# Sixty-four slots in a unit of its own for the fourth 128-slot expert, another order of the units, and biases added to the sum one unit later

## The chip, the cores and the metric

The kernel runs on one core of one Trainium2 chip, as one launch. The metric is the device time in microseconds (us); three runs of a kernel make a median. The profiled execution has its own time, and a span from its first to its last instruction.

## The reference, cut to what matters

One layer: a mixer (attention heads and a gated linear recurrence), a layer norm, then a mixture of 32 experts of which each token takes four, and a last layer norm. Sixteen meta tokens are prepended and dropped at the end, so the experts see 256 tokens here.

```python
def moe(h, w_router, b_router, w_gu, b_gu, w_dn, b_dn):
    logits = (h @ w_router) + b_router
    top_val, top_idx = lax.top_k(logits, TOP_K)          # 4 of 32
    gates = jax.nn.softmax(top_val, axis=-1)
    ...
    def expert_block(args):
        gu = xb @ w_gu[e] + b_gu[e]                      # 1024 -> 2048
        gate = jnp.minimum(gu[:, 0::2], SWIGLU_LIMIT)
        up = jnp.clip(gu[:, 1::2], -SWIGLU_LIMIT, SWIGLU_LIMIT)
        act = (up + 1.0) * gate * jax.nn.sigmoid(gate * SWIGLU_ALPHA)
        return act @ w_dn[e] + b_dn[e]                   # 1024 -> 1024
    ...
    return jnp.einsum('tkd,tk->td', y_assign, gates)
```

The weights are float32: 1024x2048 and 1024x1024 for each expert, 12.6 MB, or 403 MB for all 32.

## The kernel before

The mixer takes the first 200 us or so. Then come the experts, in a fixed list of units (`UNITS`). A place in that list is a rank: ranks 0 and 1 are experts 0 and 1 (their weights are fetched before the router is known), and ranks 2 to 31 are the other 30 experts sorted by how many tokens chose them, the fullest first. Each rank has a fixed number of slots, one for each token that chose it. A unit is 128 slots, shared by its ranks: one rank with 128 slots, two with 64 or four with 32. For a unit, `one_hots` builds a matrix of which token stands in which slot and gathers the tokens with matmuls (`gather`, L716), `slot_gates` weighs and transposes that matrix (L733), the experts run one after another (`expert128`, `expert64`, `expert32`), and in the next unit's first expert `combine` (L897, L898) adds the weighted result to the sum `acc`. Gather and slot gates of the next unit are issued inside the last expert of a unit.

Every expert reads its weights in six chunks of 2 MB, four for gate and up and two for down, and all chunks are issued from SP's queue in the order in which TensorE uses them (`chunk`, L310). They land in a ring of nine buffers, and an issue waits until TensorE has read the last of the chunk that held the buffer nine chunks earlier. So the transfers run up to nine chunks, one expert and a half, ahead of TensorE, and stop when TensorE falls too far behind. TensorE's order is the order of the program text; calls such as `amid.append((4, f))` put `f` after phase 4 of an expert (phases 0 to 3 are the four chunks of gate and up, 4 the activation, 5 the middle of down).

`begin_acc` allocates `acc`, multiplies the gates with the down biases of all experts (L981, four matmuls in the text, eight in the trace, since each float32 matmul is there twice) and adds the residual (L982). Before, it stands in the second expert of unit 0, after its third chunk.

`spread` brings the rows of the last norm's gain and bias, which `begin_acc` fetches on ACT's queue, to all partitions (two matmuls each); it stands in the last experts of units 12 and 13.

If more tokens chose an expert than it has slots (`C_CAP`, compared in `places`), a flag in `ordi` lets a loop behind the kernel's end (L1113) run such experts again with 128 slots, twice, and write the output again.

Of the kernel before, what the change touches and what calls it, by code (L numbers as in the profile page):

```python
# [16 lines left out]
OP = mybir.AluOpType  # L17
PSUM = mybir.MemoryType.PSUM if hasattr(mybir, "MemoryType") else bass.MemoryType.PSUM

P = 128  # L20
D = 1024
T = 256
# [18 lines left out]
C_CAP = C_SEL + 2 * 2  # L41
# [39 lines left out]
mix 0 4, split 35, close, prefetch 1, mix 0 5, mix 1 5, mix 0 6, mix 0 7, mix 1 6  # L81
"""


NS = 2
UNITS = [(0, 1), (28, 29, 30, 31), (2,), (18, 19), (16, 17), (3,), (14, 15), (24, 25, 26, 27), (4,), (12, 13), (10, 11),
         (5,), (8, 9), (20, 21, 22, 23), (6, 7)]


def constants():  # L90
    c = np.zeros((P, NC_CONST), np.float32)
    i = np.arange(P)
    c[:, C_ID:C_ID + P] = np.eye(P)
    c[:, C_TRI:C_TRI + P] = i[:, None] < i[None, :]
    c[:, C_ONE:C_ONE + P] = 1.0
    c[:, C_IOTA:C_IOTA + NE] = np.arange(NE)
    c[:, C_IOTA1:C_IOTA1 + P] = np.arange(1, P + 1)
    e = np.arange(NE)
    key = np.where(e < NS, 1e6 - e, NE - 1 - e)
    c[:, C_KC] = key[i % NE]  # L100
    c[:, C_KC + 1] = 6 * (i % NE)
    c[:, C_KR:C_KR + NE] = key
    for j in range(2):
        c[:, C_GRP + j] = i // NE % 2 == j
        for r in range(NS):
            c[:, C_SEL + j * NS + r] = (i // NE % 2 == j) & (i % NE == r)
    for unit in UNITS:
        for r in unit:
            c[:, C_CAP + r] = P // len(unit)
    x = np.zeros((P, NC_MIX), np.float32)  # L110
    rot = np.zeros((P, P), np.float32)
    for m in range(2):
        for j in range(32):
            rot[m * 64 + j, m * 64 + 32 + j] = -1.0
            rot[m * 64 + 32 + j, m * 64 + j] = 1.0
    x[:, E_ROT:E_ROT + P] = rot.T
    pos = np.arange(L, dtype=np.float32)
    inv = (1.0 / (np.float32(10000.0) ** (np.arange(0, 64, 2, dtype=np.float32) / np.float32(64)))).astype(np.float32)
    ang = (pos[:, None] * inv[None, :]).astype(np.float32)
    ang = np.concatenate([ang, ang, ang, ang], axis=1).T  # L120
    x[:, E_COS:E_COS + L] = np.cos(ang)
    x[:, E_SIN:E_SIN + L] = np.sin(ang)
    for lv, m in enumerate((1, 2, 4, 8, 16)):
        tt = np.arange(P).reshape(-1, 2, m)[:, 1].reshape(-1)
        x[:, E_MSK + lv * 64:E_MSK + lv * 64 + 64] = (
            (i[:, None] // (2 * m) == tt[None, :] // (2 * m)) & ((i[:, None] // m) % 2 == 0))
    return c, x


def build(ctx, tc, x, meta, consts_d, mixc_d, vecs_d, rows_d, win_d, wout_d, wr_d, br_d, bgu_d, bdn_d, wexp_d, out):  # L130
    nc = tc.nc
# [17 lines left out]
    def bank(tag):  # L149
        return ps.tile([P, 512], F32, name="ps_" + tag, tag=tag, bufs=4 if tag == "s" else 2)  # L150

    def t1(name, shape=(P, L), dt=F32):
        return cpool.tile(list(shape), dt, name=name, tag="t1", bufs=T1)

    def t4(name, shape=(P, D), dt=F32):
        return cpool.tile(list(shape), dt, name=name, tag="t4", bufs=T4)
# [535 lines left out]
        nc.vector.scalar_tensor_tensor(gat[:, a, :], ex, zz, msk[:, a, :], op0=OP.mult, op1=OP.mult)  # L692


    def hot(pc, n):

        w = P // n
        G = t1("G", (P, 2, n, w))
        nc.vector.tensor_tensor(G, con[:, None, None, C_IOTA1:C_IOTA1 + w].to_broadcast([P, 2, n, w]),  # L699
                                pc[:, :, :, None].to_broadcast([P, 2, n, w]), op=OP.is_equal)  # L700
        return G

# [4 lines left out]

    def gather(G, amid=None):

        XT = t4("XT", (P, KT, P))  # L710
        bs = [bank("s") for _ in range(2)]
        for a in range(2):
            if a and amid:
                amid()
            for k in range(KT):
                nc.tensor.matmul(bs[k // 4][:, k % 4 * P:(k % 4 + 1) * P], h[:, a, k * P:(k + 1) * P],  # L716
                                 G[:, a].rearrange("p n w -> p (n w)"), start=(a == 0 and k % 4 == 0),
                                 stop=(a == 1 and k % 4 == 3))
        for c in range(2):
            (nc.vector.tensor_copy if c else nc.scalar.copy)(XT[:, c * 4:(c + 1) * 4, :],  # L720
                                                             bs[c].rearrange("p (k s) -> p k s", s=P))
        return XT

    def gated(G, gc, n):
        Gg = t1("Gg", (P, 2, n, P // n))
        nc.vector.tensor_tensor(Gg, G, gc[:, :, :, None].to_broadcast([P, 2, n, P // n]), op=OP.mult)
        return Gg

    def turned(Gg):

        cb = bank("g")
        for a in range(2):
            nc.tensor.transpose(cb[:, a * P:(a + 1) * P], Gg[:, a].rearrange("p n w -> p (n w)"), ident)  # L733
        C = t1("C", (P, 2, P))
        nc.vector.tensor_copy(C, cb[:, 0:T].rearrange("p (a t) -> p a t", a=2))
        return C

    def swiglu(gu):
        g = t1("g", (P, 256))
# [14 lines left out]
        nc.vector.tensor_copy(at, tr[:, 0:256].rearrange("p (c s) -> p c s", c=2))  # L754
        return at

    def bias_of(src, n):

        t = t1("sel", (P, 256), F32R)
        k = 6 if n == 4 else 2  # L760
        src = src[:, 2:4] if k == 2 and src.shape[1] == 6 else src
        nc.gpsimd.tensor_copy(t[:, 0:k * P // n].rearrange("p (j w) -> p j w", j=k), src.to_broadcast([P, k, P // n]))  # L762
        return t[:, 0:k * P // n]

    def expert64(X, Y, u, w, sel, amid=()):

# [123 lines left out]

    def combine(C, Y):
        acc = late["both"]
        for a in range(2):
            for c in range(2):
                cs = slice(c * 512, (c + 1) * 512)
                o = bank("s")
                nc.tensor.matmul(o, C[:, a, :], Y[:, cs], start=True, stop=True)  # L897
                nc.vector.tensor_tensor(acc[:, a, cs], acc[:, a, cs], o, op=OP.add)  # L898

    def dynamic(e6, parts=1):  # L900
        return lambda i: chunk(wexp_d[bass.ds(e6 + i, 1)].rearrange("a p c -> p (a c)"), parts if i > 2 else 1)
# [98 lines left out]
    total, Cs, Ys, Gs = {}, {}, {}, {}  # L1000
    coming = {0: XT}

    def one_hots(i):
        us = slice(UNITS[i][0], UNITS[i][0] + len(UNITS[i]))
        Gs[i] = hot(psms[:, :, us], len(UNITS[i]))
        coming[i] = gather(Gs[i])

    def slot_gates(i):
        us = slice(UNITS[i][0], UNITS[i][0] + len(UNITS[i]))
        Cs[i] = turned(gated(Gs[i], gats[:, :, us], len(UNITS[i])))  # L1010

    def weigh_first():
        for a in range(2):
            weigh(a)
        Gs[0] = gated(G, gat[:, :, 0:2], 2)

    def turn_first():
        gates_turn()
# [13 lines left out]

    def choose_bias(i, r):
        src = con[:, C_SEL:C_SEL + 2 * NS].rearrange("p (j r) -> p j r", j=2) if r < NS else sels
        chosen[r] = bias_of(src[:, :, r:r + 1], len(UNITS[i]))

    line = [(i, r) for i, unit in enumerate(UNITS) for r in unit]
    choose_bias(*line.pop(0))
    end = len(UNITS) - 1
    for i, unit in enumerate(UNITS):  # L1040
        XT = coming.pop(i)
        Ys[i] = t4("Y")
        for u, r in enumerate(unit):
            amid = []
            if u == 0 and i:
                amid.append((4, lambda: combine(Cs.pop(i - 1), Ys.pop(i - 1))))
            if u == 0 and i == end:
                amid.append((5, begin_total))
            if u and i == end:
                amid.append((6, lambda: end_total(0)))  # L1050
            if i in (end - 2, end - 1) and u == len(unit) - 1:
                amid.append((3, lambda: spread(i - end + 2)))
            if i == 0:
                amid += ([(0, places), (0, weigh_first), (1, turn_first), (2, places_turn), (3, sort)] if u == 0 else
                         [(2, begin_acc)])
            if u == len(unit) - 1 and i < end:
                amid += [(4, lambda: one_hots(i + 1)), (5, lambda: slot_gates(i + 1))]
            sel = chosen.pop(r)
            if line:
                j, q = line.pop(0)  # L1060
                choose_bias(j, q)
            if len(unit) == 4:
                expert32(XT, Ys[i], u, weights(r), sel, amid)
            elif len(unit) == 2:
                expert64(XT, Ys[i], u, weights(r, 4 if i == end and u else 1), sel, amid)
            else:
                expert128(XT, Ys[i], weights(r), sel, amid)
# [45 lines left out]
    with tc.If(anyv > 0):  # L1113
        with tc.For_i(0, NE, 1) as r:
            ovr = nc.values_load(ordi[0:1, bass.ds(r + NE, 1)], min_val=0, max_val=1)
            with tc.If(ovr > 0):
# [8 lines left out]
                for base in (0, P):  # L1125
                    if base:
                        nc.vector.tensor_scalar(pc, pc, float(-base), None, op0=OP.add)
                    G = hot(pc, 1)
                    XT = gather(G)
                    C = turned(gated(G, gc, 1))  # L1130
                    Y = t4("Y")
                    expert128(XT, Y, dynamic(e6), bias_of(sc, 1))
                    combine(C, Y)
        finish(lambda a, c: acc[:, a, c * 512:(c + 1) * 512])

# [43 lines left out]
```

## Time and profile before

| | us |
|---|---|
| median of 3 runs | 1148.9 (1145.93 to 1151.4) |
| time of the profiled execution | 1149.03 |
| span of the profiled execution | 1146.9 |
| TensorE busy with matmuls | 1028.2 |
| transfers, mean over the span | 374 GB/s |

The span lacks 2.1 us of the execution's own time. The profiled execution is 0.1 us over the median. Times inside the trace count from the span's start.

### The profile page before, as it was taken

How to read it: one execution, taken by the hardware profiler on the slowest of the kernel's cores; microseconds unless marked ns; L12 is line 12 of the kernel's file. 1: busy time of each engine (PE TensorE's matmuls, PEld its weight loads, DVE VectorE, ACT ScalarE, POOL GpSimd, SP SyncE). 2: the span in 40 equal slices, each digit the busy share in tenths (PEclk: the TensorE clock that was granted, in tenths of full speed). 3: DMA queues.
4: the chain of work that ended last, by engine and by line, in shares of the span. 5: the costliest groups of instructions: out<-in, count | busy, mean ns of one | idle time of the engine just before them, and what ended most of it. 6: DMA issues, size and time to landing. Idle time of an engine off the chain costs nothing.

```text
span 1146.9 us, 14789 instructions
## 1 busy us (share of the span) xinstructions
PE 1028.2 (90%) x6040; PEld 536.5 (47%) x6041; DVE 343.2 (30%) x736; ACT 177.4 (15%) x393; POOL 99.3 (9%) x91
## 2 busy tenths in 40 slices
PE   5999898999679999999999767999999999966995
PEld 5988777443224544444444323444445534422442
DVE  6685878221101321212222101222121321200124
ACT  4424463101000001110001100000101001100102
POOL 3653314000000000000000000000000000000000
PEclk9989999999889999999999888999999999977998
DMA  6653468989999999999799999999999989999994
GB/s 215 263 219 111 148 220 311 377 361 402 427 427 427 428 427 428 427 427 428 311 429 427 426 427 427 429 427 427 428 428 426 410 327 429 427 428 426 427 420 162
DMA packets 37022, 428.44 MB, mean 374 GB/s; under 512 B 4388, under 2 KB 4772, under 8 KB 12758
## 3 DMA queue, kind: packets, MB, share of 16 engines
q1 hardware_dynamic: 36322, 426.71, 89.5%
q8 instruction: 50, 0.82, 0.3%
q10 hardware_dynamic: 628, 0.74, 0.2%
q14 instruction: 22, 0.18, 0.0%
HBM read 426.38 MB, written 1.05 MB: 373 GB/s over the span
## 4 chain that ended last, share of the span: by engine, by line
PE 69%; DMA 16%; DVE 6%; ACT 1%; issue 1%; POOL 0%; DVEq 0%; ACTq 0%; POOLq 0%
PE ps_pj L779 19%; DMA wchunk<-in_wexp 16%; PE ps_pj L793 10%; PE ps_s L828 5%; PE ps_pj L836 5%; PE ps_pj L828 5%; PE ps_s L716 5%; PE ps_pj L864 4%; PE ps_pj L320 4%; PE ps_s L897 2%; PE ps_pj L876 2%; DVE acc L898 1%; PE ps_s L409 1%; PE ps_g L752 1%; PE ps_pj L774 1%
## 5 line engine op out<-in xcount | busy, mean ns | idle before, releaser
L779 PE MATMUL ps_pj<-wchunk,XT 128*64 128x512 f32 x1024 | 230.5, 597 | 1.1 <-DMA wchunk<-in_wexp 1.1
L742 DVE TENSOR_SCALAR g<-ps_pj 128x256 f32<-128x256 f32 x52 | 22.0, 424 | 507.8 <-PE ps_pj L864 222.5
L864 PE MATMUL ps_pj<-wchunk,XT 128*32 128x512 f32 x768 | 116.2, 707 | 41.0 <-DMA wchunk<-in_wexp 41.0
L779 PEld LDWEIGHTS ps_pj<-wchunk,XT 128*64 128x64 f32 x1024 | 69.2, 137 | 131.9 <-issue 129.7
L793 PE MATMUL ps_pj<-wchunk,at 128*64 128x256 f32 x1024 | 116.4, 382 | 1.1 <-DVE at L754 1.1
L743 ACT ACTIVATE sgm<-g 128x256 f32<-128x256 f32 x60 | 25.0, 417 | 524.2 <-DVE g L742 516.4
L793 PEld LDWEIGHTS ps_pj<-wchunk,at 128*64 128x64 f32 x1024 | 71.3, 137 | 40.2 <-issue 3.3
L320 PE MATMUL ps_pj<-c,whi 128*128 128x272 f32 (+1 forms) x420 | 87.2, 302 | 0.7 <-DVE c L242 0.4
L864 PEld LDWEIGHTS ps_pj<-wchunk,XT 128*32 128x32 f32 x768 | 28.0, 125 | 122.0 <-issue 65.8
L762 POOL CAST sel<-sels 128x128 fp32r<-128x128 f32 (+2 forms) x30 | 10.6, 352 | 856.9 <-DVE up L746 218.5
L716 PE MATMUL ps_s<-G,h 128*128 128x128 f32 x480 | 57.8, 278 | 15.3 <-DVE G L699 14.0
L320 PEld LDWEIGHTS ps_pj<-c,whi 128*128 128x128 f32 x420 | 70.3, 199 | 2.5 <-DVE c L242 0.8
L716 PEld LDWEIGHTS ps_s<-G,h 128*128 128x128 f32 x480 | 54.8, 192 | 27.4 <-DVE G L699 24.4
L876 PE MATMUL ps_pj<-wchunk,at 128*32 128x256 f32 x768 | 56.8, 440 | 10.7 <-issue 6.2
L320 PE MATMUL ps_pj<-c,wlo 128*128 128x272 f32 (+1 forms) x224 | 65.9, 294 | 0.0
L181 POOL TENSOR_TENSOR wlo<-wraw,whi 128x1024 fp32r<-128x1024 f32 x20 | 51.4, 2570 | 61.3 <-ACT whi L179 61.2
L836 PE MATMUL ps_pj<-wchunk,at 128*128 128x512 f32 x128 | 56.3, 592 | 0.0
L828 PE MATMUL ps_s<-wchunk,XT 128*128 128x512 f32 x128 | 55.6, 592 | 0.0
L828 PE MATMUL ps_pj<-wchunk,XT 128*128 128x512 f32 x128 | 55.6, 592 | 0.0
L897 PE MATMUL ps_s<-Y,C 128*128 128x512 f32 x112 | 51.4, 602 | 0.0
L179 ACT CAST whi<-wraw 128x1024 fp32r<-128x1024 f32 x36 | 37.6, 1047 | 61.5 <-PE ps_pj L320 23.5
L876 PEld LDWEIGHTS ps_pj<-wchunk,at 128*32 128x32 f32 x768 | 29.4, 126 | 34.4 <-issue 17.3
(293 smaller groups left out, 966.6 us busy)
## 6 DMA issues: line engine op xcount, KB each, us to landing
wchunk<-in_wexp SPq DMA_DIRECT2D x189, 2048.0 KB, 21.7
wraw<-in_win SPq DMA_DIRECT2D x28, 512.0 KB, 3.7
wchunk<-in_wexp SPq DMA_DIRECT2D x12, 512.0 KB, 18.6
wraw<-in_wout SPq DMA_DIRECT2D x8, 512.0 KB, 5.5
h<-in_x SPq DMA_DIRECT2D x4, 256.0 KB, 3.1
braw<-in_bgu SPq DMA_DIRECT2D x1, 512.0 KB
eg<-in_rows SPq DMA_DIRECT2D x1, 512.0 KB, 4.5
eb<-in_rows SPq DMA_DIRECT2D x1, 512.0 KB
```

The costliest lines, as they stand in the source:

```text
L179: nc.scalar.copy(hi, raw)
L181: eng.tensor_tensor(lo, raw, hi.bitcast(F32), op=OP.subtract)
L320: nc.tensor.matmul(b[:, 0:n], w[:, ks], v[:, L - n:L], start=(k == 0 and j == 0), stop=(k == KT - 1 and j == 2))
L716: nc.tensor.matmul(bs[k // 4][:, k % 4 * P:(k % 4 + 1) * P], h[:, a, k * P:(k + 1) * P], G[:, a].rearrange("p n w -> p (n w)"), start=(a = ...
L743: nc.scalar.activation(sgm, g, AF.Sigmoid, scale=1.702)
L779: nc.tensor.matmul(gu[ab * 64:(ab + 1) * 64, :], X[:, kh * 4 + k, u * SL:(u + 1) * SL], wv[:, k, ab * 512:(ab + 1) * 512], start=False, st ...
L793: nc.tensor.matmul(dn[c][ab * 64:(ab + 1) * 64, 0:256], aTs[f // 4][:, f % 2, f // 2 % 2 * 64:f // 2 % 2 * 64 + 64], wv[:, f, ab * 256:(ab ...
L828: nc.tensor.matmul(gus[ab], X[:, kh * 4 + k, :], wv[:, k, ab * 512:(ab + 1) * 512], start=False, stop=(kh == 1 and k == 3))
L836: nc.tensor.matmul(dn[c], aT[f // 2][:, f % 2, :], wv[:, f, :], start=(f == 0), stop=(f == KT - 1))
L864: nc.tensor.matmul(gu[q * 32:(q + 1) * 32, :], X[:, kh * 4 + k, us], wv[q // 2][:, k, q % 2 * 512:(q % 2 + 1) * 512], start=False, stop=(k ...
L876: nc.tensor.matmul(dn[q * 32:(q + 1) * 32, 0:256], at[:, f % 2, f // 2 * 32:(f // 2 + 1) * 32], wv[q // 2][:, f, q % 2 * 256:(q % 2 + 1) * ...
L897: nc.tensor.matmul(o, C[:, a, :], Y[:, cs], start=True, stop=True)
```

## The change

`UNITS` now names the slots of each rank apart from how many ranks are in the unit. Rank 5, the fourth fullest of the sorted ones, had 128 slots and now has 64, alone in its unit; that unit's other 64 slots do not exist, so gather, transposes and combine work on 64 rows or columns. The units stand in another order, and `begin_acc` moves to the first expert of unit 1, ahead of that expert's `combine`.

```diff
-UNITS = [(0, 1), (28, 29, 30, 31), (2,), (18, 19), (16, 17), (3,), (14, 15), (24, 25, 26, 27), (4,), (12, 13), (10, 11),
-         (5,), (8, 9), (20, 21, 22, 23), (6, 7)]
+UNITS = [(64, (0, 1)), (32, (28, 29, 30, 31)), (128, (2,)), (64, (18, 19)), (64, (16, 17)), (64, (14, 15)), (64, (12, 13)),
+         (64, (5,)), (64, (10, 11)), (128, (3,)), (64, (8, 9)), (32, (24, 25, 26, 27)), (128, (4,)),
+         (32, (20, 21, 22, 23)), (64, (6, 7))]
...
-    for unit in UNITS:
-        for r in unit:
-            c[:, C_CAP + r] = P // len(unit)
+    for w, unit in UNITS:
+        c[:, C_CAP + np.array(unit)] = w
...
+        ns = G.shape[2] * G.shape[3]
...
-                nc.tensor.matmul(bs[k // 4][:, k % 4 * P:(k % 4 + 1) * P], h[:, a, k * P:(k + 1) * P],
+                nc.tensor.matmul(bs[k // 4][:, k % 4 * P:k % 4 * P + ns], h[:, a, k * P:(k + 1) * P],
...
-                nc.tensor.matmul(o, C[:, a, :], Y[:, cs], start=True, stop=True)
+                nc.tensor.matmul(o, C[:, a, :], Y[0:C.shape[0], cs], start=True, stop=True)
...
             if i == 0:
-                amid += ([(0, places), (0, weigh_first), (1, turn_first), (2, places_turn), (3, sort)] if u == 0 else
-                         [(2, begin_acc)])
+                amid += [(0, places), (0, weigh_first), (1, turn_first), (2, places_turn), (3, sort)] if u == 0 else []
+            if i == 1 and u == 0:
+                amid.insert(0, (2, begin_acc))
...
-            if len(unit) == 4:
+            if w == 32:
                 expert32(XT, Ys[i], u, weights(r), sel, amid)
-            elif len(unit) == 2:
+            elif w == 64:
                 expert64(XT, Ys[i], u, weights(r, 4 if i == end and u else 1), sel, amid)
```

Counted by the slots of a rank, the units stood and stand like this (64+64 is a pair, 4x32 four experts):

| unit | 0 | 1 | 2 | 3 | 4 | 5 | 6 | 7 | 8 | 9 | 10 | 11 | 12 | 13 | 14 |
|---|---|---|---|---|---|---|---|---|---|---|---|---|---|---|---|
| before | pair | 4x32 | 128 | pair | pair | 128 | pair | 4x32 | 128 | pair | pair | 128 | pair | 4x32 | pair |
| now | pair | 4x32 | 128 | pair | pair | pair | pair | 64 alone | pair | 128 | pair | 4x32 | 128 | 4x32 | pair |

On TensorE, in the second expert of unit 0 (L779 is gate and up of a 64-slot expert, L793 its down) and the first expert of unit 1 (L864 and L876 the same of a 32-slot expert), the rows of before are these:

```order
L752 MATMUL ps_g<-con,up 128x128 x2
L981 MATMUL ps_s<-bdn,gT 128x512 x4
L779 MATMUL ps_pj<-wchunk,XT 64x512 x8
L716 MATMUL ps_s<-G,h 128x128 x16
L752 MATMUL ps_g<-con,up 128x128 x2
L793 MATMUL ps_pj<-wchunk,at 64x256 x16
L733 MATMUL ps_g<-con,Gg 128x128 x2
L793 MATMUL ps_pj<-wchunk,at 64x256 x16
L859 MATMUL ps_pj<-bgu,sel 128x512 x2
L864 MATMUL ps_pj<-wchunk,XT 32x512 x32
L897 MATMUL ps_s<-Y,C 128x512 x4
```

And these are the rows of the change at the same place (its L715 is before's L716):

```order
L752 MATMUL ps_g<-con,up 128x128 x2
L779 MATMUL ps_pj<-wchunk,XT 64x512 x8
L715 MATMUL ps_s<-G,h 128x128 x16
L752 MATMUL ps_g<-con,up 128x128 x2
L793 MATMUL ps_pj<-wchunk,at 64x256 x16
L733 MATMUL ps_g<-con,Gg 128x128 x2
L793 MATMUL ps_pj<-wchunk,at 64x256 x16
L859 MATMUL ps_pj<-bgu,sel 128x512 x2
L864 MATMUL ps_pj<-wchunk,XT 32x512 x32
L981 MATMUL ps_s<-bdn,gT 128x512 x4
L897 MATMUL ps_s<-Y,C 128x512 x4
```

The four matmuls with the down biases have left unit 0 and stand between gate-up and combine of the first 32-slot expert.

On TensorE, the change's unit 7, the single 64-slot expert, has these rows (L715 gathers for unit 8):

```order
L774 MATMUL ps_pj<-bgu,sel 128x512
L779 MATMUL ps_pj<-wchunk,XT 64x512 x8
L752 MATMUL ps_g<-con,up 128x128 x2
L779 MATMUL ps_pj<-wchunk,XT 64x512 x8
L897 MATMUL ps_s<-Y,C 128x512 x4
L715 MATMUL ps_s<-G,h 128x128 x16
L752 MATMUL ps_g<-con,up 128x128 x2
L793 MATMUL ps_pj<-wchunk,at 64x256 x16
L733 MATMUL ps_g<-con,Gg 128x128 x2
L793 MATMUL ps_pj<-wchunk,at 64x256 x16
```

Combine of the unit before and gather for the unit after stand in the one expert here, as in a 128-slot unit. On SP's queue the rows are the same in both kernels, in number and order.

## Rows read from the trace of the kernel before

**Rows 1.** The page, parts 1 and 2: TensorE's share, then GB/s by slice.

```profile
PE 1028.2 (90%) x6040; PEld 536.5 (47%) x6041; DVE 343.2 (30%) x736; ACT 177.4 (15%) x393; POOL 99.3 (9%) x91
...
GB/s 215 263 219 111 148 220 311 377 361 402 427 427 427 428 427 428 427 427 428 311 429 427 426 427 427 429 427 427 428 428 426 410 327 429 427 428 426 427 420 162
```

**Rows 2.** Stretches of the experts' stage by engine; last column GB/s.

```profile
core 0: us, PE busy (x) PEld busy (x) DVE busy (x) ACT busy (x) POOL busy (x), PEclk, DMA share, GB/s
...
245.00:275.00 30.00, 27.91 (x210) 13.98 (x212) 8.96 (x20) 2.88 (x7) 1.04 (x3) 1.00 0.86 341
...
300.00:540.00 240.00, 217.20 (x1097) 99.14 (x1098) 46.27 (x110) 18.72 (x46) 2.10 (x6) 0.97 1.01 428
540.00:575.00 35.00, 33.88 (x130) 16.06 (x130) 10.04 (x23) 2.04 (x5) 0.29 (x1) 1.00 0.81 330
...
905.00:935.00 30.00, 28.88 (x112) 13.90 (x110) 7.22 (x17) 1.48 (x3) 0.29 (x1) 1.00 0.79 313
```

**Rows 3.** DMA issues by line: count, KB of one, median us to landing.

```profile
wchunk<-in_wexp SPq DMA_DIRECT2D x189, 2048.0 KB, 21.7
```

**Rows 4.** Waits of SP's queue, 540 to 575: us in total, times, longest.

```profile
SPq L310 <- PE ps_g L733: 15.8, 1, 15.8
SPq L310 <- PE ps_pj L836: 6.5, 1, 6.5
```

**Rows 5.** Line L310, issues from 555 to 575: time to landing.

```profile
DMA to landing us min/median/max: 7.5/8.2/11.6
```

**Rows 6.** Line L310, issues from 397 to 410 (end of unit 2).

```profile
DMA to landing us min/median/max: 14.7/15.8/16.8
```

**Rows 7.** The chain that ended last, units 3 to 6: start, us, what.

```profile
404.52 7.02 PE ps_pj L779 x32
...
419.51 3.63 PE ps_s L897 x8
...
430.84 7.02 PE ps_pj L779 x32
...
447.02 3.84 PE ps_s L716 x32
...
459.09 7.02 PE ps_pj L779 x32
...
565.94 7.02 PE ps_pj L779 x32
```

**Rows 8.** TensorE's waits from 262 to 351 (unit 1, four 32-slot experts).

```profile
PE ps_pj L864 <- DMA wchunk<-in_wexp: 12.8, 5, 3.8
```

**Rows 9.** The longest of TensorE's waits from 404 to 620 (units 3 to 6).

```profile
PE ps_s L716 <- DVE G L699: 4.7, 4, 1.2
```

**Rows 10.** The chain, second expert of unit 0 and first of unit 1.

```profile
241.82 3.63 PE ps_s L981 x8
245.45 3.61 PE ps_pj L779 x16
...
262.52 7.00 PE ps_pj L864 x64
...
277.96 18.15 DMA wchunk<-in_wexp
```

**Rows 11.** The chain, last of the 32-slot experts and the last pair.

```profile
1053.89 34.65 DMA wchunk<-in_wexp
...
1088.58 3.65 PE ps_pj L779 x16
...
1133.56 1.14 PE ps_s L1029 x2
```

**Rows 12.** Line L982, the sum's first value: duration min/median/max in ns.

```profile
L982 DVE SCALAR_TENSOR_TENSOR acc<-h,ps_s x4: 686/686/689, 242.9 to 245.5; 128x512 f32<-128x512 f32 x4
```

**Rows 13.** Stretches by engine: third and fourth 32-slot expert, then what follows.

```profile
646.00:701.00 55.00, 37.70 (x260) 12.05 (x260) 2.46 (x6) 3.32 (x9) 0.40 (x1) 0.78 1.01 428
701.00:767.00 66.00, 61.56 (x267) 31.81 (x261) 16.14 (x38) 5.29 (x12) 0.82 (x2) 1.00 1.01 427
1008.00:1063.00 55.00, 37.47 (x256) 12.37 (x260) 2.67 (x7) 3.32 (x9) 0.29 (x1) 0.75 1.01 428
1063.00:1133.00 70.00, 66.94 (x404) 29.65 (x396) 15.45 (x35) 7.71 (x19) 0.52 (x1) 1.00 0.92 384
```

More of the change, by code (lines that the diff above doesn't have):

```diff
@@ L692, in weigh, with hot @@
         nc.vector.scalar_tensor_tensor(gat[:, a, :], ex, zz, msk[:, a, :], op0=OP.mult, op1=OP.mult)
-    def hot(pc, n):
-        w = P // n
+    def hot(pc, n, w):
         G = t1("G", (P, 2, n, w))
@@ L719, in gather, with gated @@
         for c in range(2):
-            (nc.vector.tensor_copy if c else nc.scalar.copy)(XT[:, c * 4:(c + 1) * 4, :],
-                                                             bs[c].rearrange("p (k s) -> p k s", s=P))
-        return XT
-    def gated(G, gc, n):
-        Gg = t1("Gg", (P, 2, n, P // n))
-        nc.vector.tensor_tensor(Gg, G, gc[:, :, :, None].to_broadcast([P, 2, n, P // n]), op=OP.mult)
+            (nc.vector.tensor_copy if c else nc.scalar.copy)(XT[:, c * 4:(c + 1) * 4, 0:ns],
+                                                             bs[c].rearrange("p (k s) -> p k s", s=P)[:, :, 0:ns])
+        return XT
+    def gated(G, gc):
+        Gg = t1("Gg", G.shape)
+        nc.vector.tensor_tensor(Gg, G, gc[:, :, :, None].to_broadcast(G.shape), op=OP.mult)
         return Gg
@@ L731, in turned @@
         cb = bank("g")
+        ns = Gg.shape[2] * Gg.shape[3]
         for a in range(2):
-            nc.tensor.transpose(cb[:, a * P:(a + 1) * P], Gg[:, a].rearrange("p n w -> p (n w)"), ident)
+            nc.tensor.transpose(cb[0:ns, a * P:(a + 1) * P], Gg[:, a].rearrange("p n w -> p (n w)"), ident)
         C = t1("C", (P, 2, P))
-        nc.vector.tensor_copy(C, cb[:, 0:T].rearrange("p (a t) -> p a t", a=2))
-        return C
+        nc.vector.tensor_copy(C[0:ns], cb[0:ns, 0:T].rearrange("p (a t) -> p a t", a=2))
+        return C[0:ns]
     def swiglu(gu):
@@ L755, in act_turn, with bias_of @@
         return at
-    def bias_of(src, n):
+    def bias_of(src, w):
         t = t1("sel", (P, 256), F32R)
-        k = 6 if n == 4 else 2
+        k = 6 if w == 32 else 2
         src = src[:, 2:4] if k == 2 and src.shape[1] == 6 else src
-        nc.gpsimd.tensor_copy(t[:, 0:k * P // n].rearrange("p (j w) -> p j w", j=k), src.to_broadcast([P, k, P // n]))
-        return t[:, 0:k * P // n]
+        nc.gpsimd.tensor_copy(t[:, 0:k * w].rearrange("p (j w) -> p j w", j=k), src.to_broadcast([P, k, w]))
+        return t[:, 0:k * w]
     def expert64(X, Y, u, w, sel, amid=()):
@@ L1001, in build, with span @@
     coming = {0: XT}
+    def span(i):
+        return slice(UNITS[i][1][0], UNITS[i][1][-1] + 1)
     def one_hots(i):
-        us = slice(UNITS[i][0], UNITS[i][0] + len(UNITS[i]))
-        Gs[i] = hot(psms[:, :, us], len(UNITS[i]))
+        Gs[i] = hot(psms[:, :, span(i)], len(UNITS[i][1]), UNITS[i][0])
         coming[i] = gather(Gs[i])
     def slot_gates(i):
-        us = slice(UNITS[i][0], UNITS[i][0] + len(UNITS[i]))
-        Cs[i] = turned(gated(Gs[i], gats[:, :, us], len(UNITS[i])))
+        Cs[i] = turned(gated(Gs[i], gats[:, :, span(i)]))
     def weigh_first():
@@ L1014, in weigh_first @@
             weigh(a)
-        Gs[0] = gated(G, gat[:, :, 0:2], 2)
+        Gs[0] = gated(G, gat[:, :, 0:2])
     def turn_first():
@@ L1034, in choose_bias @@
         src = con[:, C_SEL:C_SEL + 2 * NS].rearrange("p (j r) -> p j r", j=2) if r < NS else sels
-        chosen[r] = bias_of(src[:, :, r:r + 1], len(UNITS[i]))
-    line = [(i, r) for i, unit in enumerate(UNITS) for r in unit]
+        chosen[r] = bias_of(src[:, :, r:r + 1], UNITS[i][0])
+    line = [(i, r) for i, (_, unit) in enumerate(UNITS) for r in unit]
     choose_bias(*line.pop(0))
     end = len(UNITS) - 1
-    for i, unit in enumerate(UNITS):
+    for i, (w, unit) in enumerate(UNITS):
         XT = coming.pop(i)
@@ L1127, in build @@
                         nc.vector.tensor_scalar(pc, pc, float(-base), None, op0=OP.add)
-                    G = hot(pc, 1)
+                    G = hot(pc, 1, P)
                     XT = gather(G)
-                    C = turned(gated(G, gc, 1))
+                    C = turned(gated(G, gc))
                     Y = t4("Y")
-                    expert128(XT, Y, dynamic(e6), bias_of(sc, 1))
+                    expert128(XT, Y, dynamic(e6), bias_of(sc, P))
                     combine(C, Y)
```

## Prediction, made before the changed kernel ran

> **What bounds the kernel now.** I began with the page. TensorE is busy for 90% of the span, which looks like the bound, but the row of GB/s below it says more: from the eleventh slice on it stands at 427 or 428, with two dips, 311 in slice 20 and 410, 327 in slices 32 and 33, and a slow start of 377, 361, 402 in slices 8 to 10 [rows 1]. The question for the experts' stage is therefore not how busy TensorE is, but when the stream of weights runs and when it stops.
>
> The stretches give the size of the stops [rows 2]. The level is 428 GB/s from 300 to 540. From 540 to 575 it is 330, so 35 x (1 - 330/428) = 8.0 us of stream are lost. From 905 to 935 it is 313: 30 x (1 - 313/428) = 8.1 us. From 245 to 275 it is 341: 30 x (1 - 341/428) = 6.1 us. TensorE is busy nearly throughout in all three. The waits of SP's queue say who stops the stream in the first: the issue of the next chunk waits for TensorE, 15.8 us at one go behind the long down half of the 128-slot expert [rows 4]. The ring is full of chunks that TensorE has not read.
>
> Elsewhere it is the other way round. In unit 1 TensorE waits 12.8 us for chunks [rows 8]; in units 3 to 6 no transfer is among its waits, and the longest in total is the 4.7 us for DVE's one-hot matrix [rows 9]. The chain has stretches of transfers in the 32-slot units only [rows 10, 11]. So TensorE falls behind in 128-slot units, catches up a little in pairs and wholly in 32-slot units. Its delay is harmless until it fills the ring; from there on every microsecond is lost to the stream, and the stream is what sets the end: the last chain of TensorE starts at 1088.58 with a chunk that landed [rows 11].
>
> **The budget of a unit.** An expert is six chunks of 2048 KB [rows 3], 12.58 MB, which at 428 GB/s is 29.4 us. From the chain [rows 7]: a pair takes TensorE 459.09 - 404.52 = 54.57 us, against 58.8 us of stream, so it catches up 4.2. The stretch from 404.52 to 565.94 holds two pairs and the 128-slot unit 5, so this unit takes 161.42 - 2 x 54.57 = 52.3 us, against 29.4: it falls behind by 22.9.
>
> How much the ring bears comes from the time from issue to landing. While the stream starves, it falls to 7.5 us [rows 5], so that is a transfer with nothing ahead of it. At the end of unit 2, which began with TensorE waiting for chunks [rows 8], the shortest is 14.7 us [rows 6]. So after unit 2 there are 14.7 - 7.5 = 7.2 us of slack. Now test this on what happened: units 3 and 4 add 2 x 4.2 = 8.4, unit 5 takes 22.9, and 7.2 + 8.4 - 22.9 = -7.3 us. The trace shows 8.0 lost there. The arithmetic holds to 0.7 us.
>
> **The change part by part.**
>
> *Unit order and the smaller place.* After unit 2 with its 7.2 us of slack there are now four pairs (+16.9 at 4.23 each), the single 64-slot expert, one pair (+4.2) and then the 128-slot unit (-22.9). The single expert has no row before. Its nearest are the two halves of a pair: the second takes 459.09 - 430.84 = 28.25 us and holds a gather of 3.84, and the first holds a combine of 3.63 [rows 7]. The single one holds both: 28.25 + 3.63 = 31.9 us, from above. From below, the gather for it (in the expert ahead of it) works on 64 columns in place of 128; if that halves the time, 1.9 us go. It costs -2.5 to -0.6 us of slack. I take 31.9, since the weights of those matmuls are as large as before. The slack after unit 9 is then 7.2 + 16.9 - 2.5 + 4.2 - 22.9 = 2.9 us, up to 4.8. It stays positive, so the loss of 8.0 goes. A pair follows and then a 32-slot unit, in which TensorE waits for the stream again.
>
> The last 128-slot unit, 12, now stands between two 32-slot units. It starts as unit 2 did, with TensorE waiting, so 7.2 us of slack should be left at its end; one of the two `spread` steps (two matmuls) stands in it and is covered by them. The loss of 8.1 goes too. Unit 13 then has to catch up 22.9 us; before, unit 7 had as much to catch up, after a 128-slot unit and a pair and a full ring, and was waiting for chunks by its third expert: from 646 to 701 TensorE is busy for 37.7 of 55 us [rows 13]. So the last pair begins from the stream, as before. TensorE's granted clock goes between its two levels, 1.2 and 2.4 GHz, in such waits, with means of 0.78 and 0.75, and is back at 1.00 in the 128-slot unit from 701 and in the last pair from 1063 [rows 13]. Since each of these again follows four 32-slot experts, I count nothing for the clock; if the lower level reached into the last pair, the end would come later by half of that stretch, since no cover is left there.
>
> *`begin_acc`.* Its eight matmuls take 3.63 us of TensorE [rows 10] in the second expert of unit 0, where TensorE holds the ring (6.1 us lost right behind it). Taking them out lets the chunks behind be issued 3.6 us earlier. Bounds: nothing, if another wait there holds the issue, and 6.1, the whole loss. I take 3.6. In its new place the same 3.63 us and the four DVE additions of 0.69 us ahead of that expert's activation [rows 12] delay the first 32-slot expert, which is 3.6 us earlier by then; the unit's 12.8 us of waiting for chunks hide it [rows 8]. Without that cover it would cost 3.6 us. Combine waits for the additions of `acc`, on which nothing else hangs. The two small row transfers move on ACT's queue and are read only near the end.
>
> *The rest.* Chunks, their number and their order on SP's queue are unchanged. Copies, transposes, bias masks on GpSimd and the combine of 64 rows are as many instructions as for any unit; they lie beside the stream.
>
> **Sum.** Against the profiled execution's 1149.0 us (0.1 over the median): 8.0 + 8.1 + 3.6 = 19.7, which gives 1129.3 us.
>
> **The rivals.**
>
> *A. The ring still fills in unit 9.* Slack of 2.9 us is little. If the single expert, or each of the pairs, takes some microseconds more than their rows say, what is over 2.9 is lost one for one, at most the 8.0 that is lost now. With 4 us lost: 1133; with all: 1137. Against it: the same 54.57 us for a pair and 29.4 us for an expert's stream gave back the 8.0 us lost in unit 5 to within 0.7.
>
> *B. Only the stretches move.* If TensorE were the true bound, and the waits for chunks only its own lateness, the order would be worth nothing and only the shorter place would count: 52.3 - 31.9 = 20.4 us, or 1128.6. Its time is hardly another, so its chance counts with the forecast; the waits of 12.8 us and the level of 428 speak against it.
>
> *C. No stop to win back.* Where weights come slowly enough, TensorE never fills the ring, and an order of units that empties it is worth nothing: 1149, within a few us. The trace speaks against it: 428 GB/s, and SP waiting for TensorE [rows 2, 4]. The Trainium skill has a rule of this kind, on the page "DMA: Bandwidth & Descriptors", section "Where 436 GB/s comes from": for transfers between HBM and SBUF the HBM's share of a core, some 358 GB/s, binds. As an estimate from that page's figure an expert would take 35.1 us to stream, a pair would catch up 15.7 us in every 54.6, the two dips would not exist, and the change would bring nothing there: 1149. The measured 428 GB/s decides against it; the same page measured 425 with one core alone.
>
> *D. An overflow, slower.* If rank 5 holds more than 64 tokens, the loop at L1113 runs its expert twice: 12 chunks of 4.9 us, 58.8 us, and the final norm again, which took 12.2 us, from the last matmul's end at 1133.56 + 1.14 = 1134.7 [rows 11] to the span's end at 1146.9: at least 71 on top of 1129.3, or 1200. It decides at token 65. Computed from the reference's own inputs, the counts of ranks 2 to 7 are 91, 61, 61, 52, 47, 42: rank 5 has 52. Only a router that differs by 13 tokens would do it.
>
> *E. The stream keeps a stop.* If the losses came from something that returns at the same rate wherever the units stand, the time stays within 3 us of 1149. The fit of -7.3 to 8.0 speaks against it.
>
> **How the numbers follow.** A difference of 0.5%, 5.7 us, is about what a measurement of this kernel can tell from none: under 1143.2 counts as faster, over 1154.6 as slower. The forecast with B: 0.83, between 1126.8 (all 22.2 us of the three losses won back) and 1132.9 (nothing from `begin_acc`). A: 0.09, 1131 to 1137. E: 0.04. C: 0.01. D: 0.02, and 0.01 for anything else that is slower. The range of 1126 to 1137 takes in the forecast's bounds and A. Faster 0.92, same 0.05, slower 0.03.
>
> **What would show it.** Right: the level of 428 GB/s holds without a dip from about 265 us to the last chunks; the shortest time to landing in unit 9 is about 10 us, above 7.5; the last pair's chain still begins at a landed chunk, near 1069; L981 lies behind the first 32-slot expert's gate-up, with transfers waited for later in that unit. Wrong: a dip behind unit 9 (A), a single expert of more than 35 us, TensorE waiting nowhere for chunks (B), or a second final norm (D). A last pair that starts late without waiting for a chunk would mean that unit 13 does not catch up.

## The result, and the profile after

The changed kernel takes 1134.04 us (median of 4 runs, 1132.42 to 1134.61); beside it the kernel before took 1150.15. The ratio is 0.9863, with a 95% interval of 0.9839 to 0.9886, so 13 to 19 us less. Forecast were 1129.3 us in a range of 1126 to 1137, and 19.7 us less. The direction and the places are right, and the size is about four us too large: the measured time lies above the forecast's own bounds (1126.8 to 1132.9) and inside the range only by the part that was allowed for rival A.

The profiled execution has a span of 1132.8 us, 14.1 less than before [rows 1, 2]. The page of the changed kernel, TensorE's share and GB/s by slice (a slice is 28.3 us now):

```profile
PE 1012.0 (89%) x6066; PEld 529.6 (47%) x6067; DVE 338.9 (30%) x725; ACT 177.2 (16%) x394; POOL 99.2 (9%) x91
...
GB/s 213 271 216 111 157 223 285 341 422 391 430 426 427 429 427 427 427 428 426 429 426 429 426 426 431 426 418 421 429 426 429 426 428 427 426 428 429 426 419 130
```

The slices of 311 and 327 [rows 1] are gone. Small marks of 418 and 421 are left from 736 to 793 us, at the end of unit 9 and behind it. Stretches of the changed kernel, columns as in [rows 2], last GB/s:

```profile
245.00:275.00 30.00, 28.81 (x194) 14.26 (x191) 9.65 (x20) 2.88 (x7) 0.69 (x2) 1.00 0.95 389
300.00:540.00 240.00, 219.28 (x1189) 99.16 (x1183) 48.60 (x113) 19.81 (x49) 2.29 (x7) 0.97 1.01 427
540.00:725.00 185.00, 180.03 (x992) 84.70 (x988) 39.02 (x92) 16.33 (x41) 1.87 (x6) 0.98 1.01 427
...
750.00:775.00 25.00, 25.00 (x88) 9.59 (x88) 3.39 (x8) 1.00 (x2) 0.62 (x2) 1.00 0.99 412
...
905.00:935.00 30.00, 27.85 (x139) 14.10 (x138) 4.99 (x12) 2.87 (x7) 0.00 (x0) 1.00 1.01 428
```

Where 330 and 313 stood, 427 and 428 stand now, and 341 has become 389. How close unit 9 comes to a stop is read from the time to landing of the chunks issued from 753 to 768 (line L310 is L309 here):

```profile
DMA to landing us min/median/max: 9.8/10.8/11.9
```

Starved transfers took 7.5 us [rows 5], so 2.3 us of slack are left; the prediction's sum had 2.9. TensorE's waits from 402 to 817, units 3 to 10, have no transfer in them, as in [rows 9]:

```profile
PE ps_s L715 <- DVE G L697: 9.2, 8, 1.2
PE ps_pj L823 <- ACT Y L799: 0.4, 1, 0.4
```

Pieces of the chain that ended last (start, us, what): the down biases and the combine behind them in the first 32-slot expert, the gather for the single expert, that expert's first gate-up matmuls and those of the expert behind it, and the chunk ahead of the last pair:

```profile
267.92 3.63 PE ps_s L981 x8
271.54 3.65 PE ps_s L897 x8
...
609.11 5.10 PE ps_s L715 x32
...
624.35 7.02 PE ps_pj L779 x32
...
656.15 7.02 PE ps_pj L779 x32
...
1038.65 35.72 DMA wchunk<-in_wexp
...
1074.41 3.65 PE ps_pj L779 x16
```

The last pair again starts from a landed chunk, at 1074.41 in place of 1088.58 [rows 11], 14.2 us earlier; from there to the span's end both kernels take 58.4 us. So all that the change wins or loses lies ahead of that chunk, and the landings of the chunks tell where.

The unbroken stream's pace is one chunk in 4.895 us, the median gap between the landings of neighbouring chunks in the trace. The next table, worked out from the landing of each chunk (counted from 0 in the order of their issue), gives for some chunks by how many us they landed later than chunk 31 plus 4.895 us for each chunk since. Chunk 31 lies in unit 1, where TensorE waits; chunk 183 is the one ahead of the last pair.

```
chunk                    73    88   104   145   160   183
before                  1.5   9.4   9.4  11.0  19.0  19.0
before, second profile  1.5   9.4   9.8  11.4  19.3  19.3
changed                 1.6   1.6   3.1   4.8   4.8   6.3
changed, second profile 1.5   3.1   3.1   4.6   6.1   6.1
```

Before, the stream loses 7.9 us between chunks 73 and 88 and 8.0 between 145 and 160: these are the two stops, as large as forecast (8.0, 8.1). But the stream that never stops still loses 6.1 to 6.3 us, in steps of about 1.5. The kernel before has only two such steps outside its stops (31 to 73, 104 to 145), that is 3.1 us; the other two seem to fall into its stops and cost nothing more there. So taking the stops away is worth 19.0 - 6.3 = 12.7 us (about 13 by the second profiles), and not 16.1.

The rest of the 14.1 us in these two profiles: from chunk 10 to chunk 23, where `begin_acc` was, the landings take 70.9 us before and 67.6 now, 3.3 less. And chunk 10 lands at 217.3 in place of 215.4, 1.9 us later. 12.7 + 3.3 - 1.9 = 14.1.

### The profile page after: what moved, and what is told of

Read it like the earlier page. It is cut to its first block, busy times and chain, and to the rows that moved or that the text cites. A ratio compares the mean times of both kernels' runs of the same rounds, so it can differ in the third digit from the quotient of the medians.

```text
span 1132.8 us, 14823 instructions
## 1 busy us (share of the span) xinstructions
PE 1012.0 (89%) x6066; PEld 529.6 (47%) x6067; DVE 338.9 (30%) x725; ACT 177.2 (16%) x394; POOL 99.2 (9%) x91
## 4 chain that ended last, share of the span: by engine, by line
PE 70%; DMA 16%; DVE 6%; ACT 1%; issue 1%; POOL 0%; DVEq 0%; ACTq 0%; POOLq 0%
PE ps_pj L779 20%; DMA wchunk<-in_wexp 16%; PE ps_pj L793 11%; PE ps_s L715 5%; PE ps_pj L864 4%; PE ps_pj L319 4%; PE ps_s L828 4%; PE ps_pj L836 4%; PE ps_pj L828 4%; PE ps_s L897 3%; PE ps_pj L876 2%; PE ps_g L752 1%; PE ps_pj L774 1%; PE ps_s L408 1%; DVE acc L898 1%
## 5 line engine op out<-in xcount | busy, mean ns | idle before, releaser
L779 PE MATMUL ps_pj<-wchunk,XT 128*64 128x512 f32 x1088 | 245.2, 597 | 2.1 <-DMA wchunk<-in_wexp 2.1
L864 PE MATMUL ps_pj<-wchunk,XT 128*32 128x512 f32 x768 | 110.9, 678 | 37.2 <-DMA wchunk<-in_wexp 37.2
L779 PEld LDWEIGHTS ps_pj<-wchunk,XT 128*64 128x64 f32 x1088 | 73.4, 137 | 139.9 <-issue 136.2
L793 PE MATMUL ps_pj<-wchunk,at 128*64 128x256 f32 x1088 | 125.5, 386 | 1.1 <-DVE at L754 1.1
L793 PEld LDWEIGHTS ps_pj<-wchunk,at 128*64 128x64 f32 x1088 | 76.5, 138 | 43.7 <-issue 4.9
L864 PEld LDWEIGHTS ps_pj<-wchunk,XT 128*32 128x32 f32 x768 | 27.1, 120 | 114.1 <-issue 63.0
L876 PE MATMUL ps_pj<-wchunk,at 128*32 128x256 f32 x768 | 60.4, 460 | 16.4 <-DMA wchunk<-in_wexp 7.5
L715 PE MATMUL ps_s<-G,h 128*128 128x128 f32 (+1 forms) x480 | 61.3, 289 | 15.2 <-DVE G L697 13.9
L715 PEld LDWEIGHTS ps_s<-G,h 128*128 128x128 f32 x480 | 58.2, 201 | 27.6 <-DVE G L697 24.8
L897 PE MATMUL ps_s<-Y,C 128*128 128x512 f32 (+1 forms) x112 | 51.5, 602 | 0.0
L876 PEld LDWEIGHTS ps_pj<-wchunk,at 128*32 128x32 f32 x768 | 29.4, 130 | 43.5 <-issue 21.4
L799 ACT COPY Y<-ps_pj 64x256 f32<-64x256 f32 x68 | 24.9, 366 | 147.0 <-PE ps_pj L793 146.6
L319 PEld LDWEIGHTS ps_pj<-c,wlo 128*128 128x128 f32 x224 | 44.0, 197 | 0.0
L836 PE MATMUL ps_pj<-wchunk,at 128*128 128x512 f32 x96 | 42.2, 593 | 0.0
## 6 DMA issues: line engine op xcount, KB each, us to landing
wchunk<-in_wexp SPq DMA_DIRECT2D x12, 512.0 KB, 17.5
```

Source lines behind the costliest of these rows:

```text
L319: nc.tensor.matmul(b[:, 0:n], w[:, ks], v[:, L - n:L], start=(k == 0 and j == 0), stop=(k == KT - 1 and j == 2))
L715: nc.tensor.matmul(bs[k // 4][:, k % 4 * P:k % 4 * P + ns], h[:, a, k * P:(k + 1) * P], G[:, a].rearrange("p n w -> p (n w)"), start=(a == ...
L779: nc.tensor.matmul(gu[ab * 64:(ab + 1) * 64, :], X[:, kh * 4 + k, u * SL:(u + 1) * SL], wv[:, k, ab * 512:(ab + 1) * 512], start=False, st ...
L793: nc.tensor.matmul(dn[c][ab * 64:(ab + 1) * 64, 0:256], aTs[f // 4][:, f % 2, f // 2 % 2 * 64:f // 2 % 2 * 64 + 64], wv[:, f, ab * 256:(ab ...
L799: nc.scalar.copy(Y[u * 64:(u + 1) * 64, c * 512 + ab * 256:c * 512 + (ab + 1) * 256], dn[c][ab * 64:(ab + 1) * 64, 0:256])
L836: nc.tensor.matmul(dn[c], aT[f // 2][:, f % 2, :], wv[:, f, :], start=(f == 0), stop=(f == KT - 1))
```

## Experiments

**The parts apart.** First `begin_acc` alone, in the kernel before:

```diff
-                amid += ([(0, places), (0, weigh_first), (1, turn_first), (2, places_turn), (3, sort)] if u == 0 else
-                         [(2, begin_acc)])
+                amid += [(0, places), (0, weigh_first), (1, turn_first), (2, places_turn), (3, sort)] if u == 0 else []
+            if i == 1 and u == 0:
+                amid.insert(0, (2, begin_acc))
```

> The kernel before with begin_acc in unit 1 and nothing else changed. Stream theory (the stream of weights sets the end, and a delay of TensorE costs only where it fills the ring): the stop at 245 to 275 us shrinks by the 3.6 us of the moved matmuls, the two later dips stay as they were; about 3.5 us under the kernel before. Rival (the stop at the start has another cause, or what is won there is lost again in a dip): no change, within 1 us.

Ratio to the kernel before 0.9946 (0.9927 to 0.9965), 4 to 8 us less, more than the 3.5 expected. Then the same edit taken back in the changed kernel:

> The changed kernel with begin_acc back in the second expert of unit 0. Stream theory: both dips are gone, the stop at the start is as large as before; about 15.5 us under the kernel before and 3.5 us over the changed one. Rival: as fast as the changed kernel, if the move of begin_acc is worth nothing.

Ratio 0.9858 (0.9834 to 0.9882): no difference from the changed kernel can be told from the times, where 3.5 us were expected. The stretch from 245 to 275 of the two kernels, the first with the move and the second without:

```profile
245.00:275.00 30.00, 27.91 (x200) 14.21 (x200) 10.70 (x22) 2.88 (x7) 1.04 (x3) 1.00 0.95 392
```

```profile
245.00:275.00 30.00, 27.91 (x220) 14.18 (x220) 8.47 (x19) 2.88 (x7) 1.04 (x3) 1.00 0.87 342
```

The rate follows the place of `begin_acc`, 392 and 342 as 389 and 341 in the two kernels of the change. From chunk 10 to 23 the three profiles with the biases in unit 0 take 70.9, 71.1 and 71.0 us; the nine with them in unit 1 take 67.2 to 69.1. The move is worth about 2 to 4 us where it acts. That the times of the second run don't show it lies within their interval of 5.5 us.

**Order without the smaller place, and the place without the order.** One number in `UNITS`, in unit 7:

```diff
-         (64, (5,)), (64, (10, 11)), (128, (3,)), (64, (8, 9)), (32, (24, 25, 26, 27)), (128, (4,)),
+         (128, (5,)), (64, (10, 11)), (128, (3,)), (64, (8, 9)), (32, (24, 25, 26, 27)), (128, (4,)),
```

> The new order and the moved biases, but rank 5 keeps 128 slots. Stream theory by the budget of slack: 7.2 us after unit 2, plus 16.9 in four pairs, minus 22.9 in unit 7, plus 4.2, minus 22.9 in unit 9: 17.5 us short, so one dip of about 17 us behind unit 9 and none later; some 17 us over the changed kernel, as slow as the kernel before. Rival (TensorE's work sets the end, so only the shorter place counts): 20 us over the changed kernel, with no dip.

Ratio 0.9983 (0.9963 to 1.0004), some 14 us over the changed kernel. The stretch of its stop, behind unit 9:

```profile
745.00:800.00 55.00, 53.89 (x192) 24.16 (x192) 15.12 (x35) 2.84 (x6) 0.64 (x2) 1.00 0.73 287
```

One stop of 55 x (1 - 287/428) = 18.1 us, where the budget of slack said 17.5. The rival had no stop. In time the 14 us fall short of the 17 expected. Now the old order (in the new notation), with the single 64-slot unit where unit 11 was:

```diff
-         (32, (24, 25, 26, 27)), (128, (4,)), (64, (12, 13)), (64, (10, 11)), (128, (5,)), (64, (8, 9)),
+         (32, (24, 25, 26, 27)), (128, (4,)), (64, (12, 13)), (64, (10, 11)), (64, (5,)), (64, (8, 9)),
```

> The old order with rank 5 at 64 slots alone where its 128 stood (unit 11), and the moved biases. Stream theory: the dip behind unit 5 stays with its 8 us, the one behind unit 11 is gone; about 8 us over the changed kernel, so some 1142. Rival (only the shorter place counts, wherever it stands): as fast as the changed kernel, 1134.

Ratio 0.9906 (0.9876 to 0.9936), 7 to 14 us under the kernel before and some 5 over the changed one, where 8 were expected. The intervals of the two overlap, but measured on the same chip its four runs (1138.0 to 1143.1) all lie above the five of the kernel with the units alone (1134.0 to 1136.0). Its two stretches:

```profile
540.00:575.00 35.00, 33.88 (x137) 15.37 (x137) 7.95 (x17) 1.59 (x3) 0.64 (x2) 1.00 0.81 327
905.00:935.00 30.00, 30.00 (x160) 12.18 (x158) 6.36 (x14) 2.30 (x6) 0.35 (x1) 1.00 1.01 427
```

One stop has stayed, the other is gone. TensorE has the same work as in the changed kernel, so the order alone is worth the first stop. By the landings, chunk 183 is 12.4 us late here and 6.3 in the changed kernel: 6.1 us for a stop of 8: with one stop there are three steps of 1.5 outside it, with none four. Neither part alone does it: the order without the place makes the stops one large one.

**Is TensorE's work still worth something?** The changed kernel with one more place made smaller, in unit 9:

```diff
-         (64, (5,)), (64, (10, 11)), (128, (3,)), (64, (8, 9)), (32, (24, 25, 26, 27)), (128, (4,)),
+         (64, (5,)), (64, (10, 11)), (64, (3,)), (64, (8, 9)), (32, (24, 25, 26, 27)), (128, (4,)),
```

> The changed kernel with rank 3 (61 tokens) at 64 slots as well, alone in unit 9. TensorE has some 20 us less to do. Stream theory: the stream has no stop left that this could take away, so at most the last 1 us behind unit 9 is won; 1133 to 1134 us. Rival (TensorE's work sets the end): 20 us less, some 1114 us.

1134.46 us, ratio 0.9853 (0.9824 to 0.9883), beside 0.9876 (0.9845 to 0.9907) of the changed kernel on the same chip. TensorE's share and the stretch that holds unit 9:

```profile
PE 1001.7 (88%) x6092; PEld 520.9 (46%) x6093; DVE 334.9 (30%) x714; ACT 177.2 (16%) x395; POOL 99.2 (9%) x91
```

```profile
540.00:905.00 365.00, 323.43 (x1922) 139.75 (x1920) 65.60 (x154) 30.15 (x77) 3.87 (x12) 0.93 1.01 427
```

Ten us less of busy TensorE, and the time stays: the stream has no stop left there, and it sets the end. The rival, with 1114 us, is out.

**Chance, or the change?** The changed kernel's profile has two falls of TensorE's clock that the first profile of before lacks: one from 198 to 205 us, and one at the gather for the single expert (granted clock 0.63 from 613 to 620).

> The changed kernel itself, once more. Chance theory (TensorE's clock fell to its lower level in the last gather ahead of the experts, 198 to 205 us, and in the gather for the single expert, 611 to 618 us, by chance): at least one of the two falls is absent this time, the first transfer behind the start lands near 215 us in place of 217.3, and the span is 1 to 3 us shorter where it is. Rival (the change itself makes the clock fall there): both falls are back, and the span is 1132 to 1134 us again.

1135.79 us, ratio 0.9876 (0.9845 to 0.9907). In its profile the fall at 198 to 205 us is absent, and chunk 10 lands at 215.4, 1.9 us earlier: chance. The span of 1132.0 is only 0.8 shorter: between chunks 10 and 23 the landings lose 1.2 us of it again. The fall at the gather for the single expert is back. So the gather was widened: the one-hot matrix gets 128 columns, of which the upper 64 are zero and unused.

```diff
-        Gs[i] = hot(psms[:, :, span(i)], len(UNITS[i][1]), UNITS[i][0])
+        n = len(UNITS[i][1])
+        Gs[i] = hot(psms[:, :, span(i)], n, P // n)
         coming[i] = gather(Gs[i])
+        Gs[i] = Gs[i][:, :, :, 0:UNITS[i][0]]
```

> The changed kernel, with the gather for the single expert over 128 columns, of which the expert uses 64 as before. If the narrow gather brings the clock's fall at 611 to 618 us: no fall there, the gather takes 3.8 us in place of 5.1, and behind unit 9 the stream keeps 428 GB/s; about 1 us under the changed kernel. If the fall is chance: no difference that can be told, within 1 us.

1133.09 us, ratio 0.9859 (0.9829 to 0.9888): no difference that can be told, and about 1 us was expected. The gather's group from 590 to 630, in the changed kernel, in the one with units only, and in this one:

```profile
L715 PE MATMUL ps_s<-G,h 128*128 128x64 f32 x32 | 5.1, 334 | 1.1 <-DVE G L697 1.1
```

```profile
L715 PE MATMUL ps_s<-G,h 128*128 128x64 f32 x32 | 3.8, 277 | 1.1 <-DVE G L697 1.1
```

```profile
L715 PE MATMUL ps_s<-G,h 128*128 128x128 f32 x32 | 3.8, 278 | 1.2 <-DVE G L697 1.2
```

At the full clock 64 columns take as long as 128. Of six profiles with the narrow gather three have the fall there, of the two with the wide one neither, so it is open whether narrow columns bring it. The fall costs TensorE about 3 us (31.3 for 28.2 in the expert with that gather, second of its pair). At the end of unit 9 it can be seen in the stream, in the changed kernel's second profile and with the wide gather:

```profile
750.00:775.00 25.00, 25.00 (x85) 9.57 (x83) 3.81 (x10) 1.01 (x2) 0.29 (x1) 1.00 0.95 386
```

```profile
750.00:775.00 25.00, 25.00 (x93) 9.12 (x92) 4.12 (x10) 1.42 (x3) 0.35 (x1) 1.00 1.01 428
```

With 412 in its first profile, the changed kernel moves 0.9 and 2.5 us less of transfers here. But no chunk lands later for it: at chunk 23 and at chunk 153 the landings of the changed kernel and of the one with the wide gather stand 1.5 us apart, and the second profile has no step between chunks 111 and 147. Without the fall the slack in unit 9 is larger. Issues from 748 to 766 with the wide gather:

```profile
DMA to landing us min/median/max: 12.7/13.8/14.9
```

That is 12.7 - 7.5 = 5.2 us (5.3 in the kernel with the units alone), against 2.3 with the fall. Both edits together:

> The wide gather together with rank 3 at 64 slots alone in unit 9. Stream theory: there is slack everywhere behind unit 2, so neither a fall of the clock there nor unit 9 costs anything; the same as the wide gather alone, 1132 to 1134 us. Rival (TensorE's work still counts): some 20 us less.

1134.23 us, ratio 0.9848 (0.9820 to 0.9876), as expected. No version is shown to beat the changed kernel.

**What are the steps of 1.5 us?** The idea: a chunk is in place only when each of the 16 DMA engines has moved its share. If one engine has something else to do, the chunk is late, and with no stop the engine has no chance to catch up. To test it, the changed kernel got 127 KB more, 31 partitions of `bdn` loaded again behind `begin_acc`, meant for one engine:

```diff
+        nc.scalar.dma_start(bdn[0:31], bdn_d[0:31])
```

> The changed kernel with one transfer more, from ACT's queue behind begin_acc: 31 partitions of 4 KB, 127 KB, whose result nobody reads. 31 is prime, and if the whole of it goes to one of the 16 DMA engines, at a sixteenth of 428 GB/s, that engine is 4.7 us behind the others from about 275 us on. Theory (a chunk lands when the slowest engine is done with its share, and with no stop in the stream what one engine is late stays late): the landings jump by 4 to 5 us at one chunk and the gaps of 1 us and more later become fewer, since other engines' small delays hide behind it; the end 1 to 5 us later. Rival (only the sum of the bytes counts): 0.3 us later, no jump.

1140.76 us, ratio 0.9904 (0.9870 to 0.9939), some 5 us over the changed kernel. The packets of the extra load follow one another in the trace, 31 of 0.16 us from 272.6 to 294.7, never two at once, 5.0 us in all, as they would on one engine. The stretch behind its start, then the same of the changed kernel:

```profile
285.00:305.00 20.00, 10.88 (x106) 4.26 (x104) 2.03 (x5) 1.87 (x5) 0.40 (x1) 0.90 0.71 282
```

```profile
285.00:305.00 20.00, 13.91 (x136) 5.17 (x128) 2.03 (x5) 1.87 (x5) 0.40 (x1) 0.89 1.01 430
```

Against the changed kernel chunk 23 lands 1.0 us earlier and chunk 32 5.2 us later, a jump of 6.2 us for bytes that are worth 0.3 us of the whole stream. But two causes are mixed in it. Chunks 23 to 25 land 6.5, 6.7 and 5.8 us apart in place of 4.9, together 4.3 us late, although from 272 to 284 us transfers run at 422 GB/s: bytes of later chunks move while these wait for their last share, as the idea has it. Then there is a wait of SP's queue, from 280 to 310:

```profile
SPq L309 <- DMA bdn<-in_bdn: 17.9, 1, 17.9
```

The issue of chunk 26 waited until the extra load itself had landed, so chunk 26 was issued at 295.9 us (280.6 in the changed kernel) and the stream ran dry; by chunk 30 another 3.6 us are lost. This second part is a wait in the program and says nothing of the engines. So the run shows that a small load can hold up chunks far beyond its bytes, and not that the steps come from such loads. After it there are three steps of 1.5 up to chunk 183 and not four, 4.7 us; but the changed kernel's fourth comes only at chunk 178, so that one hid behind the extra load isn't shown.

What makes the steps without this load was not tried. The program's instructions come by DMA too, 50 packets of 16 KB that take about 1.1 us each beside the weights, and the kept traces speak for them: of the 16 gaps between neighbouring landings that are 1 us or more over 4.895 (all twelve profiles, chunks 31 to 183, outside the stops, where a trace has both landings), 15 hold the start of such a packet, and of the 813 that are less than 0.35 over, 122 do. That they go together is shown; that the packets are the cause is not.

**The kernel before, once more.**

> The kernel before once more, for its profile. Stream theory: stops of some 8 us each behind units 5 and 11 and some 6 us from 245 to 275 us, as in the first profile. If the first profile was an odd one: other places or sizes.

A single run of 1154.29 us. The stops are the first profile's (table above); what differs is the start.

## Why the prediction was right, and where it was too large

- *The bound* was read rightly. The stream sets the end, TensorE's lateness counts only where it fills the ring. The second small place shows it from one side (work gone, time the same), the two half versions from the other.
- *The budget of slack* held for the stops: -7.3 forecast from the rows against 7.9 lost in unit 5; 17.5 against 18.1 in the order-only kernel. The single expert took 656.15 - 624.35 = 31.8 us from its first gate-up matmul to that of the next expert, forecast 31.9; the lower bound, a gather of half the time, was wrong, since 64 columns take as long as 128.
- *Luck in unit 9*: 2.9 us of slack forecast, 2.3 found. Without the clock's fall, which the sum didn't have, 5.2 are left. The sum also lacks the stream's own steps, 3.0 us up to there by the landings, each of which gives TensorE time to catch up; 2.9 and 2.3 lie close because the two, 3.1 and 3.0 us, nearly cancel.
- *Unit 13 catches up*, as forecast: the last pair starts from a chunk.
- *The step that failed in size* is "so the loss of 8.0 goes", and its twin of 8.1. The losses were read as bandwidth missing in a stretch, and the stops are that large (7.9 and 8.0). But what a stop takes isn't what removing it gives: the unbroken stream loses 1.5 us more in each of the two stretches. The two terms are worth 12.7 us in the profiles, 6.1 for the first alone by the place-only kernel. What the steps come from stays open.
- *`begin_acc`*: 3.3 for 3.6 us in the first profile (2.1 in the second), hidden in unit 1 as forecast.
- *Not in the sum*: the start, 1.9 us later in this profile, by chance.
- Of the rivals, A (the ring fills in unit 9) missed by 2.3 us of slack: its sign, a dip behind unit 9, is there with 412 and 386 GB/s, but no chunk lands later for it, so the time that lies in its range isn't its doing; B (only the shorter place counts) is out by the place-only kernel; C (no stop to win back) by 427 GB/s and the lost stops; D (overflow) did not occur, as no second norm is in the trace; E (a stop wherever the units stand) holds for the 1.5 us steps and for nothing larger.

## What to carry to other kernels

Where weights stream through a ring, count for each unit how much the compute gains or loses against the stream, and read the ring's slack from the shortest time to landing; order the units so that the sum never falls below zero. That foretold two stops here, of 7.9 and 18.1 us, to within a microsecond. Then take off what the unbroken stream loses anyway, measured between landings in a stretch without a stop, before calling a dip in bandwidth a gain.

## What the runs showed of the hardware that was not expected

TensorE's clock falls at different places in different executions of the same instructions, and the first 215 us carry much of the difference in span. From 190 to 215 us, the changed kernel, the last kernel with both edits, and the kernel before in its second profile (granted clock third from the end):

```profile
190.00:215.00 25.00, 20.88 (x132) 13.84 (x132) 13.35 (x50) 6.42 (x15) 7.48 (x6) 0.86 0.80 318
```

```profile
190.00:215.00 25.00, 21.02 (x132) 10.41 (x134) 11.26 (x45) 6.40 (x15) 3.74 (x5) 1.00 0.92 377
```

```profile
190.00:215.00 25.00, 21.13 (x132) 15.72 (x132) 14.12 (x51) 5.73 (x13) 8.11 (x6) 0.80 0.77 297
```

Chunk 10 lands at 217.3, 210.8 and 220.0 us in these, 215.4 in the first profile of before. The second of them had no fall in the mixer either (granted clock 1.00 from 55 to 80 and from 125 to 145 us, where the changed kernel has 0.86 and 0.91), and its span of 1125.9 us is the shortest of all; its median is not. Nine us of difference between executions thus arise ahead of chunk 10, where the change has touched nothing. What TensorE did just ahead is the same where the clock fell and where it did not: a wait of 2.2 us for DVE's router mask, in the profiles of before and of the change alike.
